# Routing of an expert layer split into two halves of tokens, and five row buffers of their own for its gathers

## The chip, the cores and the metric

The program runs on one core of one Trainium2 chip. The metric is the device time of one launch in microseconds (us). The kernel before took 3147.11 us (median of two runs, 3143.66 and 3150.56). A difference counts as faster or slower when it is over 2%.

## The reference

Two transformer blocks on 256 tokens of width 2048, in float32: a gated linear attention with its feed-forward layer, and then a hybrid attention, a memory attention and an expert layer. The change lies in the expert layer alone (`peer_ffn`). Each token picks, for each of 8 heads, 16 of 16384 experts; the layer adds up, over its 128 experts, gate times gelu of a dot product, times a row of a second table:

```
q = (xt @ w_pq).reshape(T, PEER_HEADS, 2, PEER_D_KEY // 2)
s = einsum('thpd,hpkd->thpk', q, sub_keys)
top_s, top_i = lax.top_k(s, K)                       # K = 16, of 128, twice
cand = top_s[:, :, 0, :, None] + top_s[:, :, 1, None, :]
best_s, best_c = lax.top_k(cand.reshape(T, PEER_HEADS, K * K), K)
ia, ib = top_i of the two factors at best_c // K, best_c % K
expert = ia * 128 + ib;  gate = softmax(best_s)
a = einsum('td,ted->te', xb, u_tab[eb])              # u_tab, v_tab: 16384 x 2048
out = einsum('te,ted->td', gate * gelu(a), v_tab[eb])
```

## The kernel before

**Two ways through the expert layer.** Of the 256 tokens, `ND` = 160 go the dense way: TensorE multiplies them with all of both tables, which come from HBM as 128 tiles of the u table and 128 of the v table, 1 MB each (`u_pair` takes two u tiles; a loop over `dq` and `c` takes the v tiles, one at a time). The other `NS` = 96 tokens go the gathered way: for each table, 96 indirect DMAs, of 128 rows and 1 MB each, fetch only the rows that a token picked, and VectorE (DVE) multiplies them: a dot product per row (line 1142) for the u rows, a scaled sum (lines 1148 and 1150) for the v rows. That is 192 gathers in all. Tokens 0 to 127 are the first half (`tt` = 0) and hold all gathered tokens; tokens 128 to 255 are the second half.

**The ring of table tiles.** `load_raw` (line 1041) issues tile loads on SP's queue, in order, into four buffers: `wr0`, `wr1`, `wr2` and `wl2`. A buffer is loaded again when TensorE is done with its tile. Every fourth tile thus lies in `wl2`.

**The gathers.** `gather(n)` (line 1130) issues gather n on GpSimd's (POOL's) queue into one of five buffers in turn (`NG` = 5). The name is `wh` for even n and `wl` for odd n, and the number is `n % NG // 2`, that is 0, 0, 1, 1, 2. Over ten gathers these are `wh0 wl0 wh1 wl1 wh2 wl0 wh0 wl1 wh1 wl2`: every tenth gather (n = 9, 19, ...) takes `wl2`, which is a buffer of the ring too. A step of `gathered_steps` multiplies gather n and issues gather n + 5. The steps are handed out by `raw_weight`: each table tile that TensorE takes adds `ring["rate"]` (0.83) to a credit, and each whole credit makes one step. A manual dependence holds a gather back until the matmul that was written last before it has run.

**The routing.** `lin(1, ...)` makes the query of one head, `scores(h, q)` its scores, and `route(h, ss)` the two top-16 searches (`top16`), the combination, the second search and the indices `ia` and `ib`. `route` is a generator; it is advanced by `pump` between matmuls (three steps at a time, `RATE`), so that its small instructions on DVE and POOL lie beside TensorE's work. One call of `route` handles both halves of the tokens. After the last head come one u pair, `own_rows` (the gathered tokens' own vectors), four more u pairs (`LAG`), then `drain()` ends all routing. Then the expert numbers of the first half are spread over 128 partitions (`spread`, on ScalarE's queue) and the first five gathers are issued. The gates (softmax) follow, one u pair, and three transposes of `ia`, `ib` and the gates on TensorE. From there on, for 40 u pairs, each pair also takes the gate matrices of four dense tokens: 8 small instructions on DVE (lines 1357 and 1358), 4 matmuls (`att<-Bg,sq`) and the products with what u pairs gave before.

**What sets the order.** Python's order of calls sets TensorE's order outright (`pin`). On the other engines a scheduler places instructions by a simulated timeline; each engine then runs its own list strictly in order, and each queue its own.

Two loads of the residual follow near the change from the u to the v table, on SP's queue between tile loads: `xs<-xD` (line 1397) and `xn<-xD` (line 1398), 768 KB and 1280 KB, in pieces of 384 and 640 bytes.

Of the kernel before, what the change touches and what calls it, by code (L numbers as in the profile page):

```python
# [9 lines left out]
F32 = mybir.dt.float32  # L10
F32R = mybir.dt.float32r
# [7 lines left out]
P = 128  # L19
# [10 lines left out]
NS = sum(SETS)  # L30
ND = T - NS
NE = 128
LAG = 4
RATE = 3
PER = 1
NG = 5
SHARE = 5 / 8


# [42 lines left out]
def build(tc, a, out, dbg=None):  # L82
# [4 lines left out]
    with es:  # L87
# [52 lines left out]
        def drain():  # L140
            while fillers:
                pump()
# [45 lines left out]
        def wtile(tag, i, dt=F32):  # L188
            pool = wp if i < 2 else st["ext"]
            return pool.tile([P, 2048], dt, name=tag, tag=f"{tag}{i}", bufs=1)  # L190
# [834 lines left out]
        with ExitStack() as e1:  # L1025
# [45 lines left out]
            def u_pair(rate=0):  # L1071

                ps = pl.tile([P, 2, T], F32, name="lin", tag="lin")[:, :, 0:ND]
                for i in range(2):
                    w = raw_weight(P)
                    for k in range(KT):
                        mm(ps[:, i], w[:, k], xn[:, k], k == 0, k == KT - 1)
                    if i == 0:
                        pump(rate)
                (dst, _), t = *hidden(done["tiles"], done["tiles"] + 2), done["tokens"]  # L1080
                done["tiles"] += 2
                if t:
                    g_ = gp.tile([P, 2, ND], F32, name="ga", tag="ga", bufs=2)[:, :, 0:t]
                    nc.scalar.activation(g_, ps[:, :, 0:t], AF.Gelu_apprx_tanh)
                    nc.vector.tensor_tensor(dst[:, :, 0:t], dst[:, :, 0:t], g_, ALU.mult)
                if t < ND:
                    nc.scalar.activation(dst[:, :, t:ND], ps[:, :, t:ND], AF.Gelu_apprx_tanh)
                pump(rate)
# [37 lines left out]
            def gather(n):  # L1126
                if n < len(plan):
                    t, d, m = plan[n]
                    g = fetched[n] = wtile(("wh", "wl")[n % 2], n % NG // 2, F32R).bitcast(F32)
                    ins = nc.gpsimd.indirect_dma_start(g, None, a[t], bass.IndirectOffsetOnAxis(ap=d["ix"][:, m:m + 1], axis=0))  # L1130

                    tc.add_manual_dep(ins.ins, last_pe[0], mybir.DependencyInfo(
                        mybir.DependencyClass.Sync, mybir.DependencyReason.DATA), reason="pace")
# [74 lines left out]
            with ExitStack() as e2:  # L1208
# [8 lines left out]
                def top16(vals, src, idx):  # L1217

                    s2 = rp.tile([P, P], F32, name="s2", tag="s2")[:, :src.shape[1]]
                    nc.vector.max(vals[:, 0:8], src)  # L1220
                    nc.vector.match_replace(s2, vals[:, 0:8], src, -3.0e38)  # L1221
                    nc.vector.max(vals[:, 8:16], s2)
                    nc.vector.max_index(idx[:, 0:8], vals[:, 0:8], src)
                    nc.vector.max_index(idx[:, 8:16], vals[:, 8:16], s2)

                def scores(h, q):
                    sc = pa.tile([P, 2, 2, P], F32, name="att", tag="att")
                    for p in range(2):
                        for tt in range(2):
                            mm(sc[:, p, tt], q[:, p, tt * P:tt * P + P], sk[:, 2 * h + p])  # L1230
                    ss = rp.tile([P, 2, 2, P], F32, name="ss", tag="ss", bufs=5)
                    for tt in range(2):
                        nc.scalar.activation(ss[:, :, tt], sc[:, :, tt], AF.Copy, scale=rcol[:, tt:tt + 1])
                    fillers.append(route(h, ss))

                def route(h, ss):
                    tv = rp.tile([P, 2, 2, 16], F32, name="tv", tag="tv")
                    ti = rp.tile([P, 2, 2, 16], U32, name="ti", tag="ti")
                    tf = rp.tile([P, 2, 2, 16], F32, name="tf", tag="tf")
                    for p in range(2):  # L1240
                        for tt in range(2):
                            top16(tv[:, p, tt], ss[:, p, tt], ti[:, p, tt])
                            yield
                    nc.gpsimd.tensor_copy(tf, ti)

                    cd = rp.tile([P, 2, 112], F32, name="cd", tag="cd")
                    for tt in range(2):
                        for lo, i0, i1, n in ((0, 0, 4, 16), (64, 4, 16, 4)):
                            w = (i1 - i0) * n
                            nc.vector.tensor_tensor(cd[:, tt, lo:lo + w].rearrange("p (i j) -> p i j", j=n),  # L1250
                                                    tv[:, 0, tt, i0:i1, None].to_broadcast([P, i1 - i0, n]),
                                                    tv[:, 1, tt, None, 0:n].to_broadcast([P, i1 - i0, n]), ALU.add)
                    ci = rp.tile([P, 2, 16], U32, name="ci", tag="ci")
                    for tt in range(2):
                        top16(bs[:, tt, h], cd[:, tt], ci[:, tt])
                        yield

                    cs = rp.tile([P, 2, 32], U32, name="cs", tag="cs")
                    c_ = ci.rearrange("p a k -> p (a k)")
                    for n, sh in ((0, 4), (1, 2)):  # L1260
                        nc.vector.tensor_single_scalar(cs[:, n], c_, sh, ALU.logical_shift_right)
                    sf = rp.tile([P, 2, 32], F32, name="sf", tag="sf")
                    nc.gpsimd.tensor_copy(sf, cs)
                    cf = rp.tile([P, 2, 32], F32, name="cf", tag="cf")
                    nc.gpsimd.tensor_copy(cf[:, 1], c_)
                    yield
                    nc.vector.scalar_tensor_tensor(cf[:, 0], sf[:, 1], -12.0, sf[:, 0], ALU.add, ALU.max)
                    nc.vector.tensor_scalar(sf[:, 0], cf[:, 0], 4.0, 48.0, ALU.mult, ALU.add)
                    nc.vector.scalar_tensor_tensor(sf[:, 0], cf[:, 0], 16.0, sf[:, 0], ALU.mult, ALU.min)
                    nc.vector.tensor_tensor(cf[:, 1], cf[:, 1], sf[:, 0], ALU.subtract)  # L1270
                    ee = []
                    for p in range(2):
                        e = rp.tile([P, 32, 16], F32, name="e", tag="e")
                        ee.append(e)
                        nc.vector.tensor_tensor(e, cf[:, p, :, None].to_broadcast([P, 32, 16]),
                                                iota[:, None, 0:16].to_broadcast([P, 32, 16]), ALU.is_equal)
                        for tt in range(2):
                            nc.gpsimd.tensor_tensor(e[:, 16 * tt:16 * tt + 16], e[:, 16 * tt:16 * tt + 16],
                                                    tf[:, p, tt, None, :].to_broadcast([P, 16, 16]), ALU.mult)
                    yield  # L1280
                    for e, dst in zip(ee, (ia, ib)):
                        nc.vector.tensor_reduce(dst[:, :, h], e.rearrange("p (a k) i -> p a k i", a=2),
                                                axis=mybir.AxisListType.X, op=ALU.add)

                qq = []

# [7 lines left out]
                def normed():  # L1294
                    rms(cols=rcol)
                    for dst, lo, hi in ((xn, NS, T), (xg[0], 0, NS)):
                        for k in range(KT):
                            nc.vector.scalar_tensor_tensor(dst[:, k], x[:, k, lo:hi], gains[:, 5, k:k + 1], rstd[:, lo:hi], ALU.mult, ALU.mult)

                for h in range(8):  # L1300
                    lin(1, xh, xl, evac_pq, hook=normed if h == 0 else None, rate=RATE)
                    if h >= 1:
                        scores(h - 1, qq[h - 1])
                    if st["next"] == len(order) and not loaded:
                        slots.extend(("wr", i) for i in raw_free)
                        load_raw()
# [4 lines left out]
                u_pair(RATE)  # L1311
                scores(7, qq[7])
                own_rows()
                for _ in range(LAG):
                    u_pair(RATE)
                drain()
                ef = rp.tile([P, 32, 16], F32, name="e", tag="e").rearrange("p a k -> p (a k)").rearrange("p (a k) -> p a k", k=NE)
                ei = ef[:, 1].bitcast(U32)
                nc.vector.scalar_tensor_tensor(ef[:, 0], ia[:, 0].rearrange("p h k -> p (h k)"), float(P),
                                               ib[:, 0].rearrange("p h k -> p (h k)"), ALU.mult, ALU.add)  # L1320
# [1 line left out]
                for d in sets:  # L1322
                    spread(d["ix"], ei, d, d["w"])
                next(gathered)


                gv = rp.tile([P, 16, 16], F32, name="gv", bufs=1)
# [7 lines left out]
                for d in sets:  # L1335
                    spread(d["gs"], gv.rearrange("p a k -> p (a k)"), d, d["w"])
                u_pair()
                ring["rate"] = 0.83
                for s, t in ((iaT, ia.rearrange("p a h k -> p a (h k)")), (ibT, ib.rearrange("p a h k -> p a (h k)")),
                             (gT, gv.rearrange("p (a h) k -> p a (h k)", a=2))):  # L1340
                    ps = att()
# [175 lines left out]
```

## Time and profile before

| | us |
|---|---|
| runs | 3143.66, 3150.56 (median 3147.11) |
| the profiled execution | 3146.22 |
| its span | 3144.1 |
| TensorE busy / DVE / ScalarE / POOL | 3006.3 / 1713.8 / 870.3 / 538.8 |
| expert layer, third u tile to last v tile | 1846 to 3132 |
| share of the 16 DMA engines in it | 0.92 to 0.93 |

The profile is one execution. PE is TensorE's matmul and PEld its weight load; a table tile is 16 matmuls in the program and 32 in the trace. Idle time before an instruction is put down to what ended it. SPq, ACTq and POOLq are the queues on which DMAs are issued. The trace names a buffer without its number, so that `wl` as a source of an expert matmul is always `wl2`, and `wr` is one of the other three.

### The profile page before, as it was taken

To read this page: it belongs to the slowest core of one execution; us is meant where nothing else is said; L and a number is where in the kernel's file an instruction comes from. 1 tells how busy PE (TensorE), PEld (TensorE's weight loads), DVE (VectorE), ACT (ScalarE), POOL (GpSimd) and SP (SyncE) were. 2 spreads that over 40 slices of the span, in tenths; PEclk is the share of its full clock that TensorE was granted. 3 is DMA by queue.
4 is the path that set the end of the run, shared out by engine and by line. 5 is a ranking of instruction groups with operands and counts; after the bars stand their busy time and mean duration, and the time that the engine had idled before them with its cause. 6 is when DMAs were issued, how large, how long until landed. Compare 5 with 4: busy or idle time off the path is not lost.

```text
span 3144.1 us, 52115 instructions
## 1 busy us (share of the span) xinstructions
PE 3006.3 (96%) x22786; PEld 2938.4 (93%) x22786; DVE 1713.8 (55%) x2300; ACT 870.3 (28%) x1074; POOL 538.8 (17%) x367
## 2 busy tenths in 40 slices
PE   8999999999999999999999999999989889989998
PEld 7989999999999999899998999998989889989988
DVE  6575665454545555455867885656544434344332
ACT  5335544333333444343655421111100000000001
POOL 1120012011020210000111531112222222332210
PEclk9999999999999999999999999999999989999999
DMA  5444455554555546545355559999999989999995
GB/s 191 170 147 150 160 206 183 176 200 165 200 176 197 188 161 218 184 160 177 132 184 180 198 189 405 394 356 355 378 346 399 383 328 397 401 386 400 385 378 188
DMA packets 128351, 799.50 MB, mean 254 GB/s; under 512 B 18595, under 2 KB 25676, under 8 KB 39260
## 3 DMA queue, kind: packets, MB, share of 16 engines
q1 hardware_dynamic: 99548, 593.43, 51.8%
q0 software_dynamic: 27648, 201.34, 16.0%
q8 instruction: 178, 2.92, 0.4%
q10 hardware_dynamic: 928, 1.41, 0.2%
q14 instruction: 49, 0.40, 0.0%
HBM read 790.51 MB, written 5.78 MB: 253 GB/s over the span
## 4 chain that ended last, share of the span: by engine, by line
PE 78%; DMA 10%; DVE 6%; issue 4%; POOL 1%; ACT 1%; SPq 0%; ACTq 0%; POOLq 0%; DVEq 0%
PE lin L104 72%; PE att L104 5%; DMA wl<-in_peer_v 2%; DMA wl<-in_v_rows,ix 2%; DMA wl<-in_peer_u 2%; DMA wr<-in_peer_u 1%; DMA wh<-in_v_rows,ix 1%; DMA wr<-in_peer_v 1%; DVE wl L174 1%; DVE hn L1150 1%; DVE pair L277 0%; PE att L107 0%; ACT wh L170 0%; DVE wl L1142 0%; DVE s L1221 0%
## 5 line engine op out<-in xcount | busy, mean ns | idle before, releaser
L104 PE MATMUL lin<-pair,wh 128*128 128x256 f32 x5632 | 1013.0, 282 | 15.3 <-ACT pair L276 7.9
L104 PEld LDWEIGHTS lin<-pair,wh 128*128 128x128 f32 x5632 | 869.1, 190 | 21.2 <-DVE pair L277 9.9
L174 DVE TENSOR_TENSOR wl<-wr,wh 128x2048 fp32r<-128x2048 f32 (+3 forms) x316 | 658.2, 2084 | 422.3 <-ACT wh L170 422.2
L104 PE MATMUL lin<-pair,wl 128*128 128x256 f32 (+1 forms) x3200 | 852.2, 286 | 33.7 <-DMA wl<-in_peer_v 28.1
L170 ACT ACTIVATE wh<-wr 128x2048 fp32r<-128x2048 f32 (+2 forms) x316 | 557.2, 1764 | 814.9 <-PE lin L104 730.2
L104 PEld LDWEIGHTS lin<-pair,wl 128*128 128x128 f32 x3200 | 591.4, 191 | 35.5 <-DMA wl<-in_peer_v 29.1
L104 PE MATMUL lin<-xn,wr 128*128 128x160 f32 x3072 | 427.1, 299 | 3.1 <-DMA wr<-in_peer_u 2.9
L104 PEld LDWEIGHTS lin<-xn,wr 128*128 128x128 f32 x3072 | 419.3, 190 | 4.2 <-issue 2.7
L567 POOL TENSOR_TENSOR hv<-sg,gu 128x256 f32<-128x256 f32 x44 | 101.9, 2315 | 598.4 <-ACT sg L565 598.4
L104 PE MATMUL lin<-hh,wh 128*128 128x256 f32 x704 | 199.6, 284 | 2.1 <-ACT hh L170 2.1
L104 PE MATMUL lin<-xn,wl 128*128 128x160 f32 x1024 | 159.8, 318 | 43.3 <-DMA wl<-in_peer_u 43.2
L1150 DVE SCALAR_TENSOR_TENSOR hn<-wh,hs,hn 128x2048 f32<-128x2048 f32 x46 | 108.1, 2351 | 169.1 <-DMA wh<-in_v_rows,ix 168.9
L104 PE MATMUL lin<-hl,wh 128*128 128x256 f32 x704 | 199.6, 284 | 0.3
L1150 DVE SCALAR_TENSOR_TENSOR hn<-wl,hs,hn 128x2048 f32<-128x2048 f32 x48 | 112.9, 2351 | 159.1 <-DMA wl<-in_v_rows,ix 158.5
L104 PE MATMUL lin<-hh,wl 128*128 128x256 f32 x704 | 199.2, 283 | 0.0
L104 PEld LDWEIGHTS lin<-xn,wl 128*128 128x128 f32 x1024 | 154.8, 206 | 45.9 <-DMA wl<-in_peer_u 45.9
L104 PE MATMUL lin<-pair,wr 128*128 128x160 f32 x1216 | 170.8, 299 | 3.7 <-DMA wr<-in_peer_v 3.6
L104 PEld LDWEIGHTS lin<-pair,wr 128*128 128x128 f32 x1216 | 166.7, 190 | 5.1 <-DMA wr<-in_peer_v 4.3
L104 PE MATMUL lin<-hid,wr 128*128 128x160 f32 x1216 | 170.6, 299 | 0.3 <-DMA wr<-in_peer_v 0.2
L104 PEld LDWEIGHTS lin<-hid,wr 128*128 128x128 f32 x1216 | 166.8, 190 | 0.8 <-DMA wr<-in_peer_v 0.8
L1185 ACT ACTIVATE acc<-xs 128x192 f32<-128x192 f32 x1 | 0.4, 362 | 579.5 <-DVE xs L1171 579.5
L1142 DVE CUSTOM_DVE_ANT_0 wh<-wh,hn 128x2048 f32<-128x2048 f32 x48 | 109.9, 2289 | 90.6 <-DMA wh<-in_u_rows,ix 90.6
(339 smaller groups left out, 4078.7 us busy)
## 6 DMA issues: line engine op xcount, KB each, us to landing
wr<-in_peer_u SPq DMA_DIRECT2D x96, 1024.0 KB, 9.5
wr<-in_peer_v SPq DMA_DIRECT2D x96, 1024.0 KB, 10.9
wr<-in_w_gu SPq DMA_DIRECT2D x88, 1024.0 KB, 4.9
wr<-in_w_dn SPq DMA_DIRECT2D x64, 704.0 KB, 4.1
wr<-in_w_in SPq DMA_DIRECT2D x32, 1024.0 KB, 4.9
wl<-in_peer_u SPq DMA_DIRECT2D x32, 1024.0 KB, 9.6
wl<-in_peer_v SPq DMA_DIRECT2D x32, 1024.0 KB, 9.3
wr<-in_w_v SPq DMA_DIRECT2D x16, 1024.0 KB, 4.9
```

The source lines that it names most:

```text
L104: pin(nc.tensor.matmul(ps, l, r, start=start, stop=stop, **kw))
L170: nc.scalar.activation(h, src, AF.Copy)
L174: eng.tensor_tensor(l[:, lo:hi], src[:, lo:hi], h.bitcast(F32)[:, lo:hi], ALU.subtract)
L567: nc.gpsimd.tensor_tensor(hv, sg, gu[:, 1], ALU.mult)
L1142: nc.vector.tensor_tensor_reduce(out=g, in0=g, in1=d["hn"], scale=1.0, scalar=0.0, op0=ALU.mult, op1=ALU.add, accum_out=h[:, m:m + 1])
L1150: nc.vector.scalar_tensor_tensor(d["y"], g, h[:, m:m + 1], d["y"], ALU.mult, ALU.add)
L1185: nc.scalar.activation(sq, src, AF.Square)
```

## The change

`ROWS` lists the five buffers of the gathers outright: `wh0 wl0 wh1 wl1 wh2`, in a cycle of five, without `wl2`. `route` is called once per head and half of the tokens; a generator `steps` advances the first half's routes and takes the second half's only when none of the first is waiting. After `own_rows` the first half is run to its end; its expert numbers are spread and five gathers issued; then follow a u pair, the setting of the rate (0.8 instead of 0.83), eight u pairs with two steps at a time instead of four with three, and the rest of the second half. Steps of the gathers begin with the fifth table tile instead of the thirteenth, and the transposes stand after 22 tiles instead of 12. Small instructions on 128 x 32 or 128 x 512 elements become two on half of that.

```diff
-LAG = 4
+LAG = 8
-NG = 5
+ROWS = [("wh", 0), ("wl", 0), ("wh", 1), ("wl", 1), ("wh", 2)]
+NG = len(ROWS)
...
-                    g = fetched[n] = wtile(("wh", "wl")[n % 2], n % NG // 2, F32R).bitcast(F32)
+                    g = fetched[n] = wtile(*ROWS[n % NG], F32R).bitcast(F32)
...
-                    ss = rp.tile([P, 2, 2, P], F32, name="ss", tag="ss", bufs=5)
                     for tt in range(2):
-                        nc.scalar.activation(ss[:, :, tt], sc[:, :, tt], AF.Copy, scale=rcol[:, tt:tt + 1])
-                    fillers.append(route(h, ss))
+                        ss = rp.tile([P, 2, P], F32, name="ss", tag=f"ss{tt}", bufs=(2, 8)[tt])
+                        nc.scalar.activation(ss, sc[:, :, tt], AF.Copy, scale=rcol[:, tt:tt + 1])
+                        routes[tt].append(route(h, tt, ss))
+
+                routes = [], []
+
+                def steps(n):
+
+                    for _ in range(n):
+                        for r in routes:
+                            while r and next(r[0], None) is None:
+                                r.pop(0)
+                            if r:
+                                break
+                        yield
...
+                fillers.append(steps(999))
                 for h in range(8):
...
                 own_rows()
-                for _ in range(LAG):
-                    u_pair(RATE)
-                drain()
-                ef = rp.tile([P, 32, 16], F32, name="e", tag="e").rearrange("p a k -> p (a k)").rearrange("p (a k) -> p a k", k=NE)
+                while routes[0]:
+                    pump()
+                ef = rp.tile([P, 2, 16, 16], F32, name="e", tag="e0")[:, 0].rearrange("p a b -> p (a b)").rearrange("p (a k) -> p a k", k=NE)
...
                 next(gathered)
+                u_pair(RATE)
+                ring["rate"] = 0.8
+                for _ in range(LAG):
+                    u_pair(RATE - 1)
+                while routes[1]:
+                    pump()
+                fillers.clear()
...
                 u_pair()
-                ring["rate"] = 0.83
```

The order of instructions shows the change at two places. In these rows a name's number tells one tile from another, not the buffer; the bracket tells whose counters the instruction waits for (`DMAHW` a plain DMA, `DMASW` a gather, `Pool` GpSimd).

SP's queue, loads of u tiles, a stretch from one load into `wl2` past the next; before:

```order
L1041 DMA wl_18755<-in_peer_u 128x2048 [waits DMAHW6_49,PE_49]
L1041 DMA wr_18776<-in_peer_u 128x2048 [waits DMAHW7_49,PE_49]
L1041 DMA wr_18818<-in_peer_u 128x2048 [waits DMAHW0_49,PE_49]
L1041 DMA wr_18839<-in_peer_u 128x2048 [waits DMAHW1_49,PE_49]
L1041 DMA wl_18884<-in_peer_u 128x2048 [waits DMAHW2_49,DVE_49,PE_49]
L1041 DMA wr_18905<-in_peer_u 128x2048 [waits DMAHW3_49,PE_49]
```

and in the change:

```order
L1042 DMA wl_19103<-in_peer_u 128x2048 [waits DMAHW6_49,PE_49]
L1042 DMA wr_19121<-in_peer_u 128x2048 [waits DMAHW7_49,PE_49]
L1042 DMA wr_19163<-in_peer_u 128x2048 [waits DMAHW0_49,PE_49]
L1042 DMA wr_19184<-in_peer_u 128x2048 [waits DMAHW1_49,PE_49]
L1042 DMA wl_19229<-in_peer_u 128x2048 [waits DMAHW2_49,PE_49]
L1042 DMA wr_19250<-in_peer_u 128x2048 [waits DMAHW3_49,PE_49]
```

Before, every third load into `wl2` (19 of 64 over both tables) waits for DVE as well, which multiplies the gathered rows that lie there. In the change no load into `wl2` waits for anything but TensorE and earlier loads.

POOL's queue, gathers 7 to 11 (gather 10 stands ahead of gather 9); before:

```order
L1130 DMA wl_18716<-in_u_rows,ix0_16752 128x2048 [waits DVE_49,PE_49]
L1130 DMA wh_18758<-in_u_rows,ix0_16752 128x2048 [waits DMASW0_49,PE_49]
L1130 DMA wh_18842<-in_u_rows,ix0_16752 128x2048 [waits DMASW1_49,DVE_49,PE_49]
L1130 DMA wl_18821<-in_u_rows,ix0_16752 128x2048 [waits DMAHW2_49,DMAHW6_49,DMASW2_49,PE_49]
L1130 DMA wl_18887<-in_u_rows,ix0_16752 128x2048 [waits DMASW3_49,PE_49]
```

and in the change, gathers 4 to 7:

```order
L1131 DMA wh_18309<-in_u_rows,ix0_16752 128x2048
L1285 TENSOR_TENSOR e_18423<-e_18423,tf_18350 128x256 [waits DVE_49]
L1275 CAST cf_18505<-ci_18471 128x16 [waits DVE_49]
L1273 CAST sf_18503<-cs_18500 128x32 [waits DVE_49]
L1275 CAST cf_18593<-ci_18581 128x16 [waits DVE_49]
L1273 CAST sf_18591<-cs_18588 128x32 [waits DVE_49,Pool_49]
L1257 CAST tf_18542<-ti_18541 128x32 [waits Pool_49]
L1131 DMA wh_18442<-in_u_rows,ix0_16752 128x2048 [waits DVE_49,PE_49]
L1285 TENSOR_TENSOR e_18511<-e_18511,tf_18432 128x256 [waits DVE_49]
L1285 TENSOR_TENSOR e_18618<-e_18618,tf_18542 128x256 [waits DVE_49,Pool_49]
L1131 DMA wl_18482<-in_u_rows,ix0_16752 128x2048 [waits DVE_49,PE_49]
L1131 DMA wh_18519<-in_u_rows,ix0_16752 128x2048 [waits DVE_49,PE_49]
```

Before, gather 9 waits for tile loads of the ring and for TensorE, and all routing stands ahead of the gathers. In the change gathers 5 to 12 stand among the casts and products (`e`) of the second half's routing and wait for DVE; none of them waits for a tile load.

On DVE, 132 small instructions of the second half's routing and 8 products of gathers (L1143) stand in the change between the cast that ends the first half's expert numbers and the last reduction of the second half; before, all routing stood ahead of that cast and all products of gathers behind it.

## Rows read from the trace of the kernel before

**Rows 1.** The page's first line.

```profile
span 3144.1 us, 52115 instructions
```

**Rows 2.** Windows: stretch, us; busy us (instructions) by engine; PE clock, DMA share, GB/s.

```profile
1846.00:2495.00 649.00, 602.62 (x4361) 598.94 (x4361) 364.02 (x783) 65.31 (x202) 134.31 (x120) 0.96 0.93 367
2495.00:3133.00 638.00, 582.11 (x4136) 577.17 (x4135) 240.53 (x150) 7.59 (x19) 146.16 (x92) 0.96 0.92 363
```

**Rows 3.** PE's waits from 1846 us on: total us, times, longest us.

```profile
PE lin L104 <- DMA wl<-in_peer_v: 51.6, 10, 17.6
PE lin L104 <- DMA wl<-in_peer_u: 43.2, 9, 12.6
PE lin L104 <- DMA wr<-in_peer_v: 3.8, 5, 1.9
```

**Rows 4.** Waits of SP's queue from 1850 us on: total us, times, longest us.

```profile
SPq L1041 <- DVE hs L1142: 131.9, 8, 19.7
SPq L1041 <- DMA wl<-in_v_rows,ix: 110.9, 9, 13.9
SPq L1041 <- DVE hn L1150: 21.8, 9, 2.4
```

**Rows 5.** The chain of waits at 1943 us: start us, us, what.

```profile
1943.30 2.20 DVE wl L1142
...
1945.57 6.14 DMA wl<-in_peer_u
...
1951.76 6.82 PE lin L104 x32
1958.58 0.89 PE att L104 x8
1959.47 8.70 PE lin L104 x64
```

**Rows 6.** PE's groups by tile from 1846 us on: count, busy us, mean ns, idle before.

```profile
L104 PE MATMUL lin<-xn,wr 128*128 128x160 f32 x3008 | 418.3, 299 | 3.1 <-DMA wr<-in_peer_u 2.9
...
L104 PE MATMUL lin<-hid,wr 128*128 128x160 f32 x1216 | 170.6, 299 | 0.3 <-DMA wr<-in_peer_v 0.2
L104 PE MATMUL lin<-xn,wl 128*128 128x160 f32 x1024 | 159.8, 318 | 43.3 <-DMA wl<-in_peer_u 43.2
...
L104 PE MATMUL lin<-hid,wl 128*128 128x160 f32 x512 | 80.2, 320 | 17.9 <-DMA wl<-in_peer_v 17.9
```

**Rows 7.** Two windows of 25 us with all DMA engines busy, columns as in Rows 2.

```profile
1900.00:1925.00 25.00, 24.88 (x186) 24.63 (x185) 14.06 (x24) 2.34 (x7) 3.82 (x4) 1.00 1.01 419
2450.00:2475.00 25.00, 22.11 (x144) 22.11 (x145) 7.29 (x8) 0.88 (x2) 2.81 (x3) 0.86 0.99 400
```

**Rows 8.** DMA issues: queue, count, KB each, median us from issue to landing.

```profile
xn<-xD SPq DMA_DIRECT2D x1, 1280.0 KB, 18.2
...
wl<-in_u_rows,ix POOLq DMA_INDIRECT x48, 10.6
xs<-xD SPq DMA_DIRECT2D x1, 768.0 KB, 9.4
```

**Rows 9.** Timeline around the first gather and the transposes: start us, us, instruction.

```profile
1874.41 0.23 DVE L1321 CAST e<-e 128x128 uint32<-128x128 f32 x1
...
1882.00 1.15 POOL L1130 DMA_INDIRECT wh<-in_u_rows,ix  x1 [8.68 <-PE lin L104]
...
1892.02 0.38 PE L107 MATMUL att<-ident,ia 128*128 128x128 f32 x2
```

**Rows 10.** DVE's groups from 1846 to 2495 us, columns as in Rows 6.

```profile
L1142 DVE CUSTOM_DVE_ANT_0 wh<-wh,hn 128x2048 f32<-128x2048 f32 x48 | 109.9, 2289 | 90.6 <-DMA wh<-in_u_rows,ix 90.6
...
L1358 DVE TENSOR_SCALAR Bg<-iota,ibT,gT 128x128 f32<-128x128 f32 x160 | 55.8, 351 | 0.0
...
L1223 DVE FIND_INDEX8 ti<-tv,ss 128x8 uint32<-128x128 f32 x8 | 2.1, 281 | 0.0
```

More of the change, by code (lines that the diff above doesn't have):

```diff
@@ L1230, in scores @@
                             mm(sc[:, p, tt], q[:, p, tt * P:tt * P + P], sk[:, 2 * h + p])
-                    ss = rp.tile([P, 2, 2, P], F32, name="ss", tag="ss", bufs=5)
                     for tt in range(2):
-                        nc.scalar.activation(ss[:, :, tt], sc[:, :, tt], AF.Copy, scale=rcol[:, tt:tt + 1])
-                    fillers.append(route(h, ss))
[L1236 to L1239, printed above, removed]
+                        ss = rp.tile([P, 2, P], F32, name="ss", tag=f"ss{tt}", bufs=(2, 8)[tt])
@@ L1240, in route, with new @@
+                def route(h, tt, ss):
+                    def new(name, shape, dt=F32):
+                        return rp.tile([P] + shape, dt, name=name, tag=f"{name}{tt}")
+                    tv, ti, tf = new("tv", [2, 16]), new("ti", [2, 16], U32), new("tf", [2, 16])
                     for p in range(2):
-                        for tt in range(2):
-                            top16(tv[:, p, tt], ss[:, p, tt], ti[:, p, tt])
-                            yield
+                        top16(tv[:, p], ss[:, p], ti[:, p])
+                        yield True
@@ L1244, in route @@
                     nc.gpsimd.tensor_copy(tf, ti)
[L1246 to L1259, printed above, removed]
+                    cd = new("cd", [112])
+                    for lo, i0, i1, n in ((0, 0, 4, 16), (64, 4, 16, 4)):
+                        w = (i1 - i0) * n
+                        nc.vector.tensor_tensor(cd[:, lo:lo + w].rearrange("p (i j) -> p i j", j=n),
+                                                tv[:, 0, i0:i1, None].to_broadcast([P, i1 - i0, n]),
+                                                tv[:, 1, None, 0:n].to_broadcast([P, i1 - i0, n]), ALU.add)
@@ L1260, in route @@
+                    ci = new("ci", [16], U32)
+                    top16(bs[:, tt, h], cd, ci)
+                    yield True
+                    cs = new("cs", [2, 16], U32)
                     for n, sh in ((0, 4), (1, 2)):
-                        nc.vector.tensor_single_scalar(cs[:, n], c_, sh, ALU.logical_shift_right)
-                    sf = rp.tile([P, 2, 32], F32, name="sf", tag="sf")
+                        nc.vector.tensor_single_scalar(cs[:, n], ci, sh, ALU.logical_shift_right)
@@ L1263, in route @@
+                    sf = new("sf", [2, 16])
                     nc.gpsimd.tensor_copy(sf, cs)
-                    cf = rp.tile([P, 2, 32], F32, name="cf", tag="cf")
-                    nc.gpsimd.tensor_copy(cf[:, 1], c_)
-                    yield
+                    cf = new("cf", [2, 16])
+                    nc.gpsimd.tensor_copy(cf[:, 1], ci)
+                    yield True
                     nc.vector.scalar_tensor_tensor(cf[:, 0], sf[:, 1], -12.0, sf[:, 0], ALU.add, ALU.max)
@@ L1270, in route @@
                     nc.vector.tensor_tensor(cf[:, 1], cf[:, 1], sf[:, 0], ALU.subtract)
-                    ee = []
+                    e = new("e", [2, 16, 16])
                     for p in range(2):
[L1273 to L1283, printed above, removed]
+                        nc.vector.tensor_tensor(e[:, p], cf[:, p, :, None].to_broadcast([P, 16, 16]),
+                                                iota[:, None, 0:16].to_broadcast([P, 16, 16]), ALU.is_equal)
+                        nc.gpsimd.tensor_tensor(e[:, p], e[:, p], tf[:, p, None, :].to_broadcast([P, 16, 16]), ALU.mult)
+                    yield True
+                    for p, dst in enumerate((ia, ib)):
+                        nc.vector.tensor_reduce(dst[:, tt, h], e[:, p], axis=mybir.AxisListType.X, op=ALU.add)
                 qq = []
```

## The prediction, as it was made

> **What bounds the kernel now.** I read the page first (the span of the profiled execution is 3144.1 us [rows 1], its own time 3146.22), then the expert layer in windows, since the change touches nothing ahead of it. There TensorE is busy for 602.6 of 649 us while it takes the u table and for 582.1 of 638 while it takes the v table [rows 2]; the reader is to see that the DMA engines are at 0.92 to 0.93 at the same time, so two resources are near their ends and a wait of one may hide a limit of the other. Which it is, the waits tell: TensorE waits 51.6 + 43.2 = 94.8 us in 10 + 9 waits, all for tiles in `wl`, while the waits for `wr` tiles of the v table come to 3.8 us [rows 3]. Three of four ring buffers are `wr`. A shortage of bandwidth would show on all four; this is one buffer. And 19 is the number of gathers in 192 that take `wl2`.
>
> SP's queue tells the rest: its tile loads are held up for 131.9 us by DVE's dot products, for 110.9 us by v gathers into `wl` and for 21.8 us by DVE's sums [rows 4]. The chain shows one turn [rows 5]: DVE's product of the row that lies in `wl2` ends at 1945.5, only then is the tile load issued, it lands 6.14 us later, and TensorE, idle for it, needs 6.82 us for the tile, where two tiles later take 8.70, that is 4.35 each. Since SP issues in order, the three `wr` loads behind stand still too, and come in a bunch afterwards.
>
> **Part 1, the buffers.** The gathers leave `wl2`, and the order shows no load into `wl2` that waits for DVE any more. Removed: the 19 waits, **-94.8 us** [rows 3].
>
> After such a wait the matmuls are slower: the granted clock is 0.96 in the mean of both tables [rows 2] but 1.00, its upper level of 2.4 GHz, in a window without a wait [rows 7]. The price by tile: 159.8 us / 1024 = 0.156 us for a `wl` matmul against 418.3 / 3008 = 0.139 for `wr` on `xn`, and 80.2 / 512 = 0.157 against 170.6 / 1216 = 0.140 on `hid` [rows 6]. That is 17.4 + 8.4 = 25.8 us on 1536 matmuls, and for all 2048 `wl` matmuls **-34 us**.
>
> **Part 2, what the transfers take back.** Without the waits TensorE asks for tiles faster. A tile takes 4.35 us and brings 1 + 0.8 transfers of 1.0486 MB. With all DMA engines busy and both queues filled, a window moved 419 GB/s [rows 7]: 1.8 x 1.0486 / 0.419 = 4.50 us. So the DMA engines become the bound by 0.155 us a tile. While gates are made (80 tiles), a pair of tiles takes 2 x 4.35 + 0.89 [rows 5], 4.79 each, and TensorE stays the bound. Steps run over 192 / 0.8 = 240 tiles; the other 160 lose **+25 us**. Bounds: nothing, if the gathers run a little behind, and 1.8 x 1.0486 / 0.400 = 4.72, so 0.37 x 160 = 59 us, at the lowest rate of a full window [rows 7]. I take 419, because that window is of undisturbed work, the other holds a wait. The old rate of 0.83 would cost 0.075 us a tile more.
>
> A page of the Trainium skill speaks against the change: "DMA: Bandwidth & Descriptors", section Specifications, gives HBM about 358 GB/s per core, and the stage as a whole moves 363 to 367 [rows 2]. By it nothing could be won, and the time would stay at 3147. The rows differ from it: 419 GB/s with this one core at work [rows 7]; so the sum goes by the rows, and the rule is a rival below.
>
> **Part 3, the change of tables.** Two of the waits, 12.6 and 17.6 us [rows 3], are longer than the other 17, which have 94.8 - 30.2 = 64.6 us, 3.8 each. They fall on the two residual loads, which take 9.4 and 18.2 us [rows 8] on SP's queue, ahead of tile loads. Their excess, 8.8 + 13.8 = 22.6 us, is not the shared buffer's doing alone. The ring will then be three tiles (13 us) ahead, so some of it will be hidden: I keep **+15 us**, between 0 and 22.6.
>
> **Part 4, the routing.** The expert numbers of the first half are ready at 1874.4 now, the first gather starts at 1882.0 [rows 9]: 7.6 us for the spread. In the change 132 small DVE instructions of the second half, at about 0.28 us [rows 10] 37 us, no longer stand ahead; against that, halved instructions cost more in number. So the gathers start up to some 30 us earlier; that moves transfers, and saves no time, since the rate is lower and the last step comes at tile 4 + 240 = 244, where before it came at 12 + 231 = 243. The price lies behind: TensorE's transposes need both halves. At the latest, with the cast still at 1874.4, the first gather lands 7.6 + 10.6 us later [rows 8], and the eighth product (2.29 us [rows 10]) follows after seven more landings 5.0 us apart (one transfer at half of 419 GB/s): 1874.4 + 18.2 + 35 + 2.3 + 2 = 1932. DVE's own work would end at 1874.4 + 37 + 8 x 2.29 = 1930. TensorE comes to the transposes ten tiles later than 1892.0 [rows 9], at 1935.5. So even then the routing is in time: **0 us**, and at worst the rival below. Of what is queued behind: ScalarE's queue holds u pairs' gelus behind the spread, but TensorE has four PSUM buffers, 8 tiles or 35 us, ahead; POOL's casts stand behind gathers that wait for DVE, which is counted in the 1932. Gates start ten tiles later and end at tile 104 of 128: 0.
>
> **The sum.** 3146.2 - 94.8 - 34 + 25 + 15 = **3057 us**. The profiled execution is 0.9 us under the median, so the median is predicted as 3057 too. Bounds of the unknown costs: 3146.2 - 128.8 = 3017 with both at nothing, and 3017 + 59 + 22.6 = 3099 with both at their ends.
>
> **The rivals.**
>
> *The DMA engines are the bound at 400 GB/s.* For: their share is above 0.9 all along. Against: TensorE's waits are on one buffer of four. Time: 3057 + (59 - 25) = 3091, waits of under 1 us on `wr` and `wl` alike. Chance 0.13.
>
> *The memory gives no more than now.* With the 363 to 367 GB/s of the stage [rows 2] as a limit, the same bytes take the same time, and the waits move from `wl` to all tiles: 3147. A window at 419 lasting 25 us speaks against it. Chance 0.04. The 358 GB/s of the Trainium skill, "DMA: Bandwidth & Descriptors", Specifications, would do this too.
>
> *The second half's routing is late.* If gathers do not overlap among POOL's casts (POOL waits for DVE, DVE for the landing), eight of them take 8 x (10.6 + 2.3) = 103 us: 1877 + 103 = 1980, TensorE would wait 44 us at the transposes, 3101. It decides once the landings lie over 5.5 us apart. Chance 0.08.
>
> *DVE becomes the bound beside the gates: slower than before.* DVE waits for landings in order (90.6 us before one of the two groups of products [rows 10]), and gate instructions, 8 per pair at 0.35 [rows 10], stand behind. If no gate work fits between landings, a pair costs DVE 1.6 x 5.0 + 2.8 + about 1.5 for the products of the gates = 12.3 us against TensorE's 9.6; 2.7 x 40 pairs = 108 us, 3165. It decides when DVE's time per pair passes 9.6 us. Against: DVE is busy for 364 of 649 us [rows 2] and TensorE has no wait for it now. Chance 0.05.
>
> *The change does not free the ring.* If the wait only moved to another shared buffer, half of the gain would be lost: about 3110. The order speaks against it. Chance 0.03.
>
> **How the numbers follow.** The forecast has 0.62, with 3028 to 3086 as its own range, and 0.05 is left for a better end below that. The first and third rival and both bounds, but for 3 us below, lie within 3020 to 3101; outside are the second, fourth and fifth rival and tails of others, some 0.18. 2%, about what a measurement of this kernel can tell from no change, is 63 us: faster is below 3084. Faster: 0.62 x 0.93 + 0.05 + a third of the first rival (0.04) + tails 0.03 = 0.70. Slower, above 3210, is a part of the DVE rival: 0.03. The rest, 0.27, is within 2%.
>
> **What would show it.** Right: no wait of TensorE for `wl` beyond what `wr` has per tile; SP's queue waits for TensorE alone; the 25 us windows of the v table at 400 GB/s and more throughout; the mean clock near 1.00; a wait of 5 to 15 us left at the change of tables. Wrong: waits at `ia` or `gv` before the transposes (routing late), waits of the gate matmuls for DVE, or many short waits on all four buffers with the DMA share at 1.0 (bandwidth).

## The result, and the profile after

The changed kernel takes 3051.09 us (median of two runs, 3050.75 and 3051.42) against 3147.11: a ratio of 0.9695, 95% interval 0.9649 to 0.9741. That is faster, 6 us below the forecast. The profiled execution took 3051.42 us, 94.8 less than that of before. Line numbers of the change are one higher than before's up to the routing, and 11 or 12 higher behind it.

PE's waits from 1834 us on answer to [rows 3]; total us, times, longest us:

```profile
PE lin L105 <- DMA wr<-in_peer_u: 13.2, 9, 10.4
PE lin L105 <- DMA wr<-in_peer_v: 11.6, 14, 6.7
PE lin L105 <- DMA wl<-in_peer_v: 3.3, 5, 1.8
PE lin L105 <- DMA wl<-in_peer_u: 1.0, 2, 0.7
```

The reader is to see three things. The waits for `wl` have gone from 94.8 to 4.3 us. Waits for `wr` have come up instead, and two of them are most of it: 10.4 us once in the u table and 6.7 at the change of tables. The rest are short waits, on all four buffers.

The waits of SP's queue from 1834 us on, against [rows 4]: no DVE line of the gathers and no `v_rows` is left, and one line stands out that has nothing to do with the ring's buffers:

```profile
SPq L1042 <- PE lin L105: 857.1, 201, 10.1
...
SPq L1042 <- DMA gs<-gv: 18.2, 2, 17.0
SPq L1042 <- DMA wl<-in_peer_u: 14.9, 2, 9.1
```

PE's groups by tile, against [rows 6], from 1846 us on: `wl` matmuls now take as long as `wr` matmuls, 299 to 301 ns in these lines.

```profile
L105 PE MATMUL lin<-xn,wr 128*128 128x160 f32 x3003 | 421.9, 301 | 14.0 <-DMA wr<-in_peer_u 13.2 <-ACT ga L1085 0.6
...
L105 PE MATMUL lin<-hid,wr 128*128 128x160 f32 x1216 | 171.8, 300 | 1.7 <-DMA wr<-in_peer_v 1.5
L105 PE MATMUL lin<-xn,wl 128*128 128x160 f32 x1024 | 144.5, 299 | 1.0 <-DMA wl<-in_peer_u 1.0
...
L105 PE MATMUL lin<-hid,wl 128*128 128x160 f32 x512 | 72.6, 300 | 0.6 <-DMA wl<-in_peer_v 0.4
```

Windows, columns as in [rows 2]: the u table, the v table, and four stretches of 25 us:

```profile
1846.00:2450.00 604.00, 589.04 (x4348) 585.81 (x4347) 392.11 (x915) 61.61 (x191) 142.35 (x145) 0.99 1.00 399
2450.00:3040.00 590.00, 572.95 (x4147) 565.29 (x4145) 234.89 (x148) 8.45 (x20) 114.09 (x88) 0.99 0.96 387
2500.00:2525.00 25.00, 25.00 (x187) 25.00 (x186) 9.06 (x4) 0.00 (x0) 4.92 (x5) 1.00 1.01 420
2800.00:2825.00 25.00, 25.00 (x189) 25.00 (x188) 15.99 (x12) 0.00 (x0) 3.73 (x4) 1.00 1.01 409
2900.00:2925.00 25.00, 24.82 (x180) 24.25 (x180) 10.24 (x5) 0.00 (x0) 5.92 (x5) 1.00 1.01 418
2970.00:2995.00 25.00, 25.00 (x189) 25.00 (x188) 6.03 (x14) 2.46 (x8) 0.00 (x0) 1.00 0.68 225
```

The granted clock is 0.99 where it was 0.96, so TensorE is at its upper level of 2.4 GHz nearly throughout, and while gathers run the DMA engines are full at 409 to 420 GB/s. When the last gather is in (its product ends at 2966.6), 225 GB/s are left, which is the ring alone. The rival that had 363 to 367 GB/s as a limit is out. The 358 GB/s of the Trainium skill ("DMA: Bandwidth & Descriptors", Specifications) does not hold for this lone core; the 425 GB/s that the same page gives under Bandwidth, measured with the other core idle, is what the trace agrees with.

For the experiments I split the expert layer in three by TensorE's timeline: the u table (first to last `xn` matmul), the v table (from there to its last matmul) and the tail. Before: 660.4, 637.4, 11.7 us. The change: 617.1, 586.4, 12.3.

### The profile page after: what moved, and what is told of

The parts are those of the page before. It is cut to its first block, busy times and chain, and to the rows that moved or that the text cites. A ratio compares the mean times of both kernels' runs of the same rounds, so it can differ in the third digit from the quotient of the medians.

```text
span 3049.6 us, 52187 instructions
## 1 busy us (share of the span) xinstructions
PE 2985.5 (98%) x22786; PEld 2915.5 (96%) x22786; DVE 1730.6 (57%) x2385; ACT 867.4 (28%) x1064; POOL 513.7 (17%) x391
## 3 DMA queue, kind: packets, MB, share of 16 engines
q0 software_dynamic: 27648, 201.34, 16.1%
## 4 chain that ended last, share of the span: by engine, by line
PE 82%; DMA 11%; DVE 5%; issue 1%; ACT 1%; POOL 1%; DVEq 0%; POOLq 0%; ACTq 0%; SPq 0%
PE lin L105 75%; PE att L105 6%; DMA wr<-in_peer_v 5%; DMA wl<-in_peer_v 2%; DMA wr<-in_peer_u 2%; DVE wl L175 1%; DMA wh<-in_u_rows,ix 1%; DMA wl<-in_peer_u 0%; DVE pair L278 0%; PE att L108 0%; ACT wh L171 0%; DVE s L1222 0%; DVE e L1283 0%; DVE ti L1225 0%; POOL hv L568 0%
## 5 line engine op out<-in xcount | busy, mean ns | idle before, releaser
L105 PEld LDWEIGHTS lin<-xn,wr 128*128 128x128 f32 x3072 | 422.3, 191 | 16.7 <-issue 13.9
L1151 DVE SCALAR_TENSOR_TENSOR hn<-wh,hs,hn 128x2048 f32<-128x2048 f32 x56 | 131.6, 2350 | 157.2 <-DMA wh<-in_v_rows,ix 157.1
L1151 DVE SCALAR_TENSOR_TENSOR hn<-wl,hs,hn 128x2048 f32<-128x2048 f32 x38 | 89.3, 2351 | 104.4 <-DMA wl<-in_v_rows,ix 104.4
L105 PE MATMUL lin<-wh,pair 128*128 128x512 f32 x448 | 146.0, 399 | 0.0
L105 PE MATMUL lin<-xn,wl 128*128 128x160 f32 x1024 | 144.5, 299 | 1.0 <-DMA wl<-in_peer_u 1.0
L105 PEld LDWEIGHTS lin<-xn,wl 128*128 128x128 f32 x1024 | 140.8, 190 | 1.5 <-DMA wl<-in_peer_u 1.5
## 6 DMA issues: line engine op xcount, KB each, us to landing
wr<-in_peer_v SPq DMA_DIRECT2D x96, 1024.0 KB, 12.7
```

What stands on the lines that cost most here:

```text
L105: pin(nc.tensor.matmul(ps, l, r, start=start, stop=stop, **kw))
L1151: nc.vector.scalar_tensor_tensor(d["y"], g, h[:, m:m + 1], d["y"], ALU.mult, ALU.add)
```

## The experiments

Each was timed beside the kernel before, which had medians of 3146 to 3150 us.

**The buffers alone.** Edit to the kernel before:

```diff
-NG = 5
+NG, ROWS = 5, [("wh", 0), ("wl", 0), ("wh", 1), ("wl", 1), ("wh", 2)]
...
-                    g = fetched[n] = wtile(("wh", "wl")[n % 2], n % NG // 2, F32R).bitcast(F32)
+                    g = fetched[n] = wtile(*ROWS[n % NG], F32R).bitcast(F32)
```

> The kernel before with one edit: the five row buffers of the gathers no longer include wl2. Routing in one piece, four u pairs, rate 0.83 as before. Theory A (the shared buffer is all of it): TensorE's waits for wl fall from 95 us to a few, wl matmuls take as long as wr matmuls; 3056 us (3046 to 3068), within 10 us of the whole change. Rival B (half or more of the gain comes from the split routing and the earlier gathers): 3095 or more. Rival C (the old rate of 0.83 costs, since the DMA engines are full): 3065 to 3075, with short waits on wr and wl alike in the v table.

Measured: 3050.74 us, ratio 0.9700 (0.9684 to 0.9716). PE's waits:

```profile
PE lin L104 <- DMA wr<-in_peer_v: 15.7, 26, 6.3
PE lin L104 <- DMA wr<-in_peer_u: 5.7, 9, 1.5
PE lin L104 <- DMA wl<-in_peer_v: 4.2, 9, 1.1
PE lin L104 <- DMA wl<-in_peer_u: 1.0, 3, 0.3
```

Two lines of the diff give the whole gain; theory A holds, B and C fall. The wait of 10.4 us in the u table is not there. Its u table takes 609.3 us, 7.8 less than the change's; its v table 593.1, 6.7 more.

**The split alone.** The same edit backwards, on the changed kernel; its rate stays at 0.8.

> The whole change, but with the old formula for the row buffers, so that every tenth gather takes wl2 again. Theory A: about 19 waits for wl come back, SP's queue waits for DVE's products, wl matmuls are slower again: 3140 us (3125 to 3160). Rival B (the split routing is the larger part): 3100 or less.

Measured: 3155.82 us, ratio 1.0035 (1.0017 to 1.0053): no gain, rather a loss. PE's waits, then SP's, from the profile of the fastest of six runs, 3141.08 us:

```profile
PE lin L104 <- DMA wl<-in_peer_u: 63.5, 10, 31.6
PE lin L104 <- DMA wl<-in_peer_v: 28.0, 11, 4.6
```

```profile
SPq L1041 <- DVE hs L1142: 164.5, 9, 34.5
...
SPq L1041 <- DMA wl<-in_v_rows,ix: 114.6, 10, 13.6
```

With gathers in `wl2` the waits are back, one of them 31.6 us long. So the shared buffer is the cause, from both sides.

**The old rate in the change.** Edit: `ring["rate"] = 0.83` for 0.8.

> The whole change with the old rate of 0.83 steps per tile instead of 0.80. Theory D (the DMA engines are the bound in the v table, 4.50 us a tile at 0.80, and 0.075 us more at 0.83, over some 140 tiles): up to +10 us, less what comes back when the gathers end 9 tiles earlier: 3056 us (3053 to 3062), with more short waits on wr and wl. Rival (the ring of four tiles hides it): 3051, within 2 us of the whole change.

Measured: 3061.32 us, ratio 0.9729 (0.9713 to 0.9746), 10.2 over the change; theory D, at the upper end. The longest lines of PE's waits:

```profile
PE lin L105 <- DMA wr<-in_peer_v: 16.8, 24, 8.5
PE lin L105 <- DMA wr<-in_peer_u: 16.8, 8, 10.9
```

The v table takes 593.2 us, as in the buffers alone (593.1, rate 0.83 too). At 417 GB/s a tile with its gathers takes 1.83 x 1.0486 / 0.417 = 4.60 us at 0.83 and 4.53 at 0.80. That is 0.075 us a tile, about 8 us over some 110 tiles of the v table with gathers; 6.8 were measured. The u table takes 622.7 us, 13.4 more than in the buffers alone at the same rate, and a wait of 10.9 us is in it. (This profile is of the slowest of the four runs, 3064.58 us.) So at one rate the split costs some 13 us in the u table and nothing in the v table; the lower rate gives back 5.6 us in the u table and 6.8 in the v table, and so the buffers alone and the whole change tie.

**The wait of 10.4 us.** The timeline of the change around it (start us, us, engine, line, operation, count, idle before):

```profile
1910.96 0.41 DVE L1342 TENSOR_TENSOR gv<-bs 128x256 f32<-128x256 f32 x1
...
1913.59 3.94 ACTq L1105 DMA_DIRECT2D gs<-gv  x6
...
1919.93 0.33 SPq L1042 DMA_DIRECT2D wr<-in_peer_u  x1
...
1927.49 7.56 PE L105 MATMUL lin<-xn,wr 128*128 128x160 f32 x32 [10.37 <-DMA wr<-in_peer_u]
```

SP issues a tile load at 1919.93, just after the gates' spread `gs<-gv` of ScalarE's queue, and by its waits it had stood 17.0 us for that spread. The two share no buffer. They share counters: in the order of the change plain DMAs take eight completion counters in turn, and one that gets a counter waits for the DMA that had it before. Four of the six spreads, and the three ring loads that stood behind them, the first of them issued at 1919.93:

```
L1105 DMA gs_16753<-gv 64x64 [waits DMAHW1_49,DVE_49]
L1105 DMA gs_16753<-gv 64x64 [waits DMAHW2_49]
L1105 DMA gs_16756<-gv 32x32 [waits DMAHW3_49]
L1105 DMA gs_16756<-gv 32x32 [waits DMAHW4_49]
...
L1042 DMA wr_18829<-in_peer_u 128x2048 [waits DMAHW7_49,DMAHW1_49,PE_49]
...
L1042 DMA wl_18869<-in_peer_u 128x2048 [waits DMAHW2_49,PE_49]
...
L1042 DMA wr_18906<-in_peer_u 128x2048 [waits DMAHW5_49,DMAHW3_49,PE_49]
```

These three need counters 1, 2 and 3, which the first three spreads hold (7 and 5 are those of the tile that lay in the buffer before). By the landing records of the trace the three spreads are complete at 1919.88, 1921.50 and 1921.92 us; the loads are issued at 1919.93, 1921.56 and 1921.99.

The spread itself waits for DVE's gates, so for the second half's routing, and that stands on DVE among products that wait for gathers. The experiment ties the spread to the last matmul of the pair after the transposes (in `spread`, `late` adds that dependence):

```diff
...
-                for d in sets:
-                    spread(d["gs"], gv.rearrange("p a k -> p (a k)"), d, d["w"])
...
                 u_pair()
+                for d in sets:
+                    spread(d["gs"], gv.rearrange("p a k -> p (a k)"), d, d["w"], late=True)
```

> The whole change, but the six small DMAs that spread the gates (gs<-gv) are held back, by a dependence on a matmul, until the transposes are over. Theory E (ring loads share the eight DMA counters with these six; the loads that come after them in the order wait until they have landed, and they wait for the gates, that is for the routing of the second half): SP's waits for gs<-gv (18 us) go, TensorE's wait of 10.4 us near 1927 falls under 3 us, 3043 us (3040 to 3047). Rival F (that wait is a burst of gathers that crowds out the ring's loads): 10 us stay, 3051. Rival G (the wait goes, but the transfers that are now earlier are waited for later in DMA-bound tiles): 3048 to 3051.

Measured: 3064.19 us, ratio 0.9745 (0.9728 to 0.9761), 13 slower than the change. Theory E has the cause right (SP's wait for `gs<-gv` and the 10.4 us are gone, and no wait for a `wr` tile of the u table is over 1.9 us) and the time wrong, because the next wait was already there (line numbers are 3 higher: L1146 is the dot product, L1372 makes the gate matrices `Bg`):

```profile
PE att L105 <- DVE Bg L1372: 20.6, 1, 20.6
...
PE lin L105 <- DMA wr<-in_peer_u: 4.9, 9, 1.9
```

```profile
1961.02 2.29 DVE L1146 CUSTOM_DVE_ANT_0 wh<-wh,hn 128x2048 f32<-128x2048 f32 x1 [1.18 <-DMA wh<-in_u_rows,ix]
...
1966.01 2.29 DVE L1146 CUSTOM_DVE_ANT_0 wl<-wl,hn 128x2048 f32<-128x2048 f32 x1 [2.69 <-DMA wl<-in_u_rows,ix]
...
1971.00 2.29 DVE L1146 CUSTOM_DVE_ANT_0 wh<-wh,hn 128x2048 f32<-128x2048 f32 x1 [2.69 <-DMA wh<-in_u_rows,ix]
...
1975.72 2.14 DVE L1372 TENSOR_SCALAR Bg<-iota,ibT,gT 128x128 f32<-128x128 f32 x8
```

Read the starts: 1961.0, 1966.0, 1971.0. The rows land 5.0 us apart, 1.0486 MB at 210 GB/s, half of what the DMA engines give while the ring takes the other half, as in Part 4. The first gate matrices stand behind these products in DVE's fixed order. That is the mechanism of the rival "DVE becomes the bound beside the gates", at the first gates only. In the change it costs nothing: while the ring stood still the gathers had the DMA engines to themselves and caught up (the trace records every DMA packet; from 1913 to 1917 us it gives them 418 GB/s and the ring nothing), and TensorE came 12 us later (transposes at 1947.9 instead of 1935.4). One wait hid the other.

**The split with both waits eased.** gs_late with three rates: 0.5 until the transposes, 0.88 beside the gates, 0.78 after.

> The split routing at its best: the whole change, the gates' spread held back as in gs_late (which lost its wait of 10.4 us for the ring but got one of 20.6 us at the first gate matrices), and rates of 0.5 up to the transposes, 0.88 beside the gates, 0.78 after. Theory M (the gate matrices Bg stood on DVE behind products whose rows land only every 5.0 us, since both queues share the DMA engines; with about 14 instead of 20 products ahead they are in time): no wait for Bg over 2 us, none of 10 us for the ring; 3040 us (3036 to 3045), the same as buf_rates (3040.5), so the split is worth nothing. Rival N (the split is worth something once its two waits are gone): under 3034. Rival O (the wait for Bg has another cause): it stays at 10 us or more, 3050 or more.

Measured: 3042.39 us, ratio 0.9666 (0.9649 to 0.9683).

```profile
PE lin L105 <- DMA wr<-in_peer_v: 14.0, 14, 9.4
PE att L105 <- DVE Bg L1372: 6.4, 1, 6.4
PE lin L105 <- DMA wl<-in_peer_v: 1.5, 4, 0.4
```

With fewer products ahead the wait for `Bg` falls from 20.6 to 6.4 us, not under 2 as expected. The 9.4 us are the wait at the change of tables. The time is that of the same late rates without the split (next). Even so the split earns nothing.

**Rates by stage, on the buffers alone.** 0.88 beside the gates, 0.78 after; and, for the rate by itself, 0.81 throughout.

> The kernel before with the five row buffers apart, and two rates: 0.88 steps a tile while gates are made (TensorE takes 4.8 us for such a tile, so the same DMA rate carries more there), 0.78 for the other tiles. Theory K (the DMA engines bind outside the gates and have room beside them): waits in the v table fall from 20 to under 12 us, 3042 us (3037 to 3047). Rival L (beside the gates DVE or the DMA engines are then the bound: gate matmuls wait for Bg, or tiles of the u table for their loads): 3051 or more.

> The kernel before with the five row buffers apart from the ring, and a rate of 0.81 instead of 0.83. The buffers alone gave 3050.7 at 0.83, the whole change 3051.1 at 0.80 and 3061.3 at 0.83. Theory I (the split routing costs 10 us through the early wait, and the lower rate gains them back: 10 us for 0.03): 3044 us (3040 to 3048). Rival J (the rate matters only beside the early gathers, or the later end of the gathers, tile 249 of 256, costs as much at the end): 3051, within 2 us.

Measured: 3040.52 us for the two rates, ratio 0.9668 (0.9646 to 0.9691), theory K: the v table takes 580.9 us, the u table 608.7. 0.81 throughout gives 3055.47, ratio 0.9715 (0.9693 to 0.9738), slower than 0.83, so theory I falls, and the time of its rival J (3051) is missed too. The late end that J names is there: the v table stays at 593.3 (more of the gathers fall into it), the last product ends at 2988.8 instead of 2963.8, and the tail grows from 12.3 to 17.7 us with a wait of 5.4 for DVE's last sums:

```profile
PE att L104 <- DVE acc L1189: 5.4, 1, 5.4
```

Steps that start at tile 12 and run at 0.81 end too near the end. What helps is to move transfers to where a tile takes TensorE longer, not to slow them down everywhere.

**Less to transfer.** Edit to the change; it leaves out every second gather of the v rows, 48 of 96, and multiplies the rows of the gather before once more:

```diff
+                    if t == "v_rows" and m % 2:
+                        fetched[n] = fetched[n - 1] if n - 1 in fetched else last_g[0]
+                        return
...
```

> The whole change, but every second gather of the v table's rows is left out (its product takes the rows of the gather before it once more): 48 MB less, 1.4 transfers a tile instead of 1.8 in the first three quarters of the v table. Theory D (the short waits in the v table are the DMA engines at their limit): nearly all waits of 0.3 to 1.8 us there go, 8 to 10 us, and the matmuls beside them run a little faster: 3038 us (3032 to 3043). The wait at the change of tables stays, 4 to 7 us. Rival (waits come from somewhere else than bandwidth): 3047 to 3051.

Measured: 3023.34 us, ratio 0.9612 (0.9590 to 0.9634), 27.8 less than the change: theory D's cause, and twice the gain that I expected. The window over most of the v table, in the change and then here:

```profile
2450.00:2960.00 510.00, 494.38 (x3570) 487.37 (x3568) 215.86 (x105) 0.44 (x1) 114.09 (x88) 0.99 1.01 414
2450.00:2960.00 510.00, 510.00 (x3761) 510.00 (x3760) 220.61 (x112) 1.67 (x5) 71.59 (x44) 1.00 0.91 335
```

TensorE is busy for all of 510 us; no wait over 0.3 us for a v tile is left, not even that at the change of tables. The v table takes 560.6 us, 25.8 less than in the change. So what is left to win there is the DMA engines', and part of it had no wait to show it: TensorE's own busy time was longer, 494.38 us for 3570 matmuls (138 ns each) against 510.00 for 3761 (136).

**The residual at the change of tables.** `xD` in two arrays, so that its loads move whole rows of 6 and 10 KB; on the change, and then on the buffers with two rates.

> The whole change, but the residual is stored in two arrays, so that the loads of xs and xn near the change of tables move whole rows of 6 and 10 KB instead of pieces of 384 and 640 bytes. Theory H (the small pieces keep SP's queue too long beside the gathers, and the ring's lead of three tiles doesn't cover it): the wait of 6.74 us at the change of tables falls under 1 us, 3044 us (3041 to 3047). Rival (the wait is the bytes' doing, 2.1 MB more in full DMA engines): 3 us or more of it stay, 3048 to 3051.

> buf_rates (buffers apart, rates 0.88 and 0.78, no split; 3040.5 us) with the residual stored in two whole arrays, as in xd_whole. In xd_whole the wait at the change of tables fell from 6.7 to 4.4 us only, and the time by 4.5. Theory H (size of the pieces): 3036 us (3033 to 3039), the wait there under 4 us. Rival P (the time saved there is waited for later, since the DMA engines are full in the v table): 3040, within 2 us.

Measured: 3046.60 us, ratio 0.9687 (0.9664 to 0.9711), and 3037.05, ratio 0.9643 (0.9626 to 0.9661); 4.5 and 3.5 less, in runs that spread over 6 us each. The waits for v tiles, whose longest is the one at the change of tables, in the one and the other:

```profile
PE lin L105 <- DMA wr<-in_peer_v: 11.9, 18, 4.4
PE lin L104 <- DMA wr<-in_peer_v: 8.7, 11, 5.0
```

That wait went from 6.7 to 4.4 us, and from 5.6 to 5.0; theory H has both times in its ranges, but not the waits. The loads' times in xd_whole:

```profile
xn<-xD SPq DMA_DIRECT2D x1, 1280.0 KB, 16.5
xs<-xD SPq DMA_DIRECT2D x1, 768.0 KB, 9.5
```

The 18.2 and 9.4 us of [rows 8] are the kernel before's. With the ring's buffers apart, the same pieces took 19.1 and 14.1 us in gs_late, 22.7 and 16.9 in rate83. The packet records of the traces show the pieces by themselves: the 1.31 MB of `xn` are 2048 packets of 640 bytes, 36 ns each, in the change, and 128 of 10240 bytes, 390 ns each, in xd_whole. That is 4.6 and 3.1 us of all 16 DMA engines, and beside the gathers the packets take 10.3 and 7.4 us from first to last. So the pieces cost some 3 us of the queue's time there, and the wait fell by 2.3 and 0.6: theory H is the smaller part, and more of the wait stays with whole rows, as its rival has it. Only `xn` lies at the change of tables. `xs` is issued 110 us earlier (2341.3 against 2451.3 in the change), and no wait for a tile after it is over 0.5 us until then.

**One buffer more for the ring.** Four row buffers, `wh2` to the ring, on the buffers with two rates; then the same with the residual in two arrays and rates of 0.90 and 0.77.

> buf_rates (3040.5 us) with one row buffer given to the ring: four buffers for the gathers (wh0, wl0, wh1, wl1), five for the tiles (wr0 to wr2, wl2, wh2). Theory Q (a lead of four tiles, 17 us, covers the change of tables and the short waits): the waits for tiles fall from 15.5 to under 6 us, 3032 us (3028 to 3038), if four gathers in flight still bring a row set every 4.9 us (landing about 12 us after issue plus a product of 2.3 us, over 4: 3.6 us). Rival R (four buffers are too few: the gathers run behind, the last ends late): the last product after 3000 us of the span, 3050 us or more. Rival S (the DMA engines' rate of 417 GB/s is the bound, not the lead): 3037 to 3042.

> ring5 (3035.9 us) with the residual in two whole arrays and rates of 0.90 beside the gates and 0.77 after. Theory T (the v table's time is 128 tiles at the larger of 4.35 us and (1 + rate) x 1.0486 MB / 417 GB/s while gathers last, plus the residual's 2.1 MB at that rate, 5.0 us): at 0.77 a tile takes 4.45 instead of 4.48 us over 120 tiles, 3 us less; whole rows instead of pieces 1 to 3 us less; 3031 us (3028 to 3035), with 4 to 5 us of wait left at the change of tables. Rival (beside the gates 1.90 transfers at 4.79 us, 416 GB/s, are already too many: TensorE waits there): 3036 or more.

Measured: 3035.87 us, ratio 0.9643 (0.9626 to 0.9660), and 3033.96, ratio 0.9634 (0.9619 to 0.9649), the shortest time of a kernel here that does all the work, 17 us under the change. The first waits of the second:

```profile
PE lin L104 <- DMA wl<-in_peer_v: 6.7, 3, 6.0
PE lin L104 <- DMA wr<-in_peer_v: 4.7, 13, 0.4
```

Four row buffers are enough (R falls), but a lead of four tiles does not cover the change of tables (6.0 us of wait, 5.6 in ring5). The time of ring5 lies in Q's range, but its waits for tiles come to 16.7 us, where Q had under 6 and the kernel without the fifth buffer has 16.1, so Q falls. This fits a ring that has no lead to spend where the DMA engines are the bound, which was not measured by itself. The last step, 1.9 us, is within the runs' spread, and its v table (582.9) did not get shorter than ring5's (579.4), against theory T.

## Why the prediction was right

**Part 1, the waits (-94.8): right.** 4.3 us of waits for `wl` are left, -90.5. Both single edits show the cause.

**Part 1, the slower matmuls (-34): right.** All `wl` groups of both tables took 321.3 us before and 289.8 now, -31.5, at a granted clock of 0.99 for 0.96.

**Part 2 (+25): right mechanism, size between 11 and 19.** Between the two traces the short waits and longer `wr` matmuls come to about 11 us: 4.3 on `wl`, 1.0 more than before on `wr` without the two long waits, and 5.9 of `wr` matmuls without the tile behind the first wait. (The short waits on all four buffers, 12.0 us in all at a DMA share of 0.96 to 1.00, are one of the signs that I had named for being wrong; they are there, but small.) Against a v table with fewer transfers it is 25.8 - 6.7 = 19 us. The rate of 417 to 419 GB/s was right, and 0.075 us a tile for the old rate was measured as 6.8 us in the v table. The rival at 400 GB/s is out.

**Part 3 (+15): 6.7.** One of the two places is right. Of the loads only `xn` lies at the change of tables, and the 6.7 us are its; behind `xs`, where I had an excess of 8.8 us, no wait is over 0.5. I took the price for queue time that the ring's lead would cover in part. The runs show queue time (10.3 us for the packets of `xn`, 7.4 in whole rows), but a lead of one tile more did not cover it (5.6 to 6.0 us left), and with half the v gathers none is left: it is the transfers in full DMA engines that make it.

**Part 4 (0): this step failed.** The routing is in time for the transposes, as worked out (gates at 1911 to 1913.6, transposes at 1947.9 without a wait), and the gathers started 13.8 us earlier (1868.2 instead of 1882.0) for nothing, as foreseen. But of the second half's late end I followed only `ia`, `ib` and the gates on TensorE, and not the six spread DMAs, which hold ring loads through the counters; that SP's queue would wait for TensorE alone was one of my signs, and it does not. Price: 10.4 us and 3.0 for the slow tile after it (7.56 against 4.51), 13.4. Such waits stood on SP before too, 12.7 us at the longest:

```profile
SPq L1041 <- DMA gs<-gv: 17.6, 2, 12.7
```

TensorE had only two waits around them, 0.6 and 1.5 us; so the waits were in the profile before, and short enough to cost next to nothing.

**The sum.** -90.5 - 31.5 gained; 13.4 + 6.7 and 1.0 + 5.9 given back (the 4.3 are in the 90.5): -95.0, measured -94.8. The forecast was -88.8: it gave back 40 us in two terms that took 18, and missed one of 13. The agreement within 6 us is partly luck, these errors against each other. (The chance of 0.03 for a time above 3210 has no way to it in the prediction: its DVE rival comes to 3165.) And most of the diff, the split routing, was worth nothing by itself.

## What to carry to other kernels

A wait on one buffer of a ring points at who else uses that buffer; when the buffer is freed, work out how far the next limit is, here the DMA engines at (1 + rate) transfers a tile, and put the transfers beside the work that is longest per tile. Starting transfers earlier gave nothing here: at the same rate of 0.83 the split's last product ended 20 us before that of the buffers alone (2943.5 against 2963.8), and the kernel took 10.6 us more. What stands behind transfers in a fixed order, or shares a completion counter with a DMA that waits for them, is late with them. When a repair costs time, look for the wait that the old one had been hiding.

## What the runs showed of the hardware

A gather of 1.0486 MB lands every 5.0 us while the ring loads too, so two busy queues get 210 GB/s each of some 419, as the packet records of gs_late have it from 1940 to 1950 us; the Trainium skill ("DMA: Bandwidth & Descriptors", Queues, rings and completion order) has each DMA engine go round its queues packet by packet, which agrees. Small pieces run slower on the same DMA engines: packets of 640 bytes at 36 ns come to some 285 GB/s over the 16, packets of 10240 bytes at 390 ns to 420.
